# A chunked scan dealt out in five steps a unit between quarters of the projections

## The chip, the cores and the metric

The kernel runs on one core of a Trainium2 chip. Its time is the device time in microseconds (us) of one execution; three runs of the kernel before gave 2012.23, 2012.35 and 2016.85 us, a median of 2012.35. Six names stand for the engines: PE (matrix multiplication; PEld is its weight load), DVE (vector), ACT (activation functions, copies), POOL (GpSimd), and SP, which here issues nearly all DMAs. Each engine takes its instructions in a fixed order, in which an instruction that waits for a semaphore holds up all behind it.

## What is computed

One layer of a hybrid decoder, x of 2048 tokens by 1024, in float32:

```
u = rms_norm(x); proj = u @ w_in          # q, k, v, z_att, f, z_ssd, xbc, dt, x_lru, z_lru
y_att = fox_attention(q, k, v, log_f) * silu(z_att)       # 8 heads of 64
y_ssd = ssd_mixer(xbc, dt, z_ssd)                         # 16 heads in 2 groups, 16 chunks of 128
y_lru = rglru(x_lru) * silu(z_lru)
out = x + concat(y_att, y_ssd, y_lru) @ w_out
# ssd, per chunk c and group g, heads e:
lmat = exp(causal(a_cs[l] - a_cs[s])); cb = C_c @ B_c^T
y_diag = (cb * lmat_e) @ (x*dt)_e ; y_off = exp(a_cs) * (C_c @ state)
state  = exp(a_tot) * state + B_c^T @ (decay * x*dt)
```

## The kernel before

The stages follow each other: normalisation and transposes of x, convolution inputs, the gated linear recurrence and z_ssd, then the stage that the change is about, then attention with the output projection filled in between its steps. Tensors that pass between stages lie in DRAM (`xs_d`, `b_d`, `bt_d`, `ct_d`, `zs_d`, `acs_d`, the results `gt_d`, and q, k, v as `qk_d`, `v_d`).

In the stage around the change two things run side by side. **The scan** has 32 units (16 chunks by 2 groups), each made by `ssd_unit`: five loads (`xs`, `zz`, `bm`, `bt`, `ct`), the product `cb` on PE, two halves `q` of four heads each (load of the decays `ab`, a mask by POOL, four exponentials by ACT, a product with `cb` by DVE, four matmuls into `py`), the matmul `po` with the state, `y` on DVE, the matmul `pn` for the next state, and `store`: four transposes `pty`, a copy `yt` and the DMA to `gt_d`. `xs`, `bm`, `bt`, `ct`, `ab` and `y` have two buffers, `zz`, `xd`, `xe`, `yo` and `yt` one; the five PSUM results of a unit share three buffers (`psY`). **The projections** are 56 steps: 32 of q and k (`pqk`, in four groups of 8, each followed by transposes `ptq`, splits `sth` and `stl` on ACT and DVE, and four stores), 8 of v (`pv`), and 16 of z (`pza`). A group's weights come through four raw buffers `wr` and are split into `wh` and `wl` (eight buffers each), so the second half of the next group's weights can only be loaded when the group in progress is nearly over. In float32r a step of q/k has 48 matmuls of 256 columns, one of z 24 of 512.

The program writes the whole scan ahead of the projections, and a list scheduler with its own time model merges the two when the program is built: it takes what it thinks is ready, earlier text first. Nothing ties a unit of the scan to a projection step. What comes after the scan (`zm`, `q3`, `k2` and their memsets in the memory that the scan leaves) is written behind it, and the loads of attention's first head (`load_head(0)`, `load_q(0)`) stand behind the third group of projections.

Of the kernel before, what the change touches and what calls it, by code (L numbers as in the profile page):

```python
# [8 lines left out]
F32 = mybir.dt.float32  # L9
F32R = mybir.dt.float32r  # L10
# [33 lines left out]
UP, DOWN = (0, 1, 2, 3, 4, 5, 6, 7), (7, 6, 5, 4, 3, 2, 1, 0)  # L44
ORD = (DOWN,) + (UP,) * 6 + (DOWN,)
XB = 7
PB = (2, 3, 2, 1)


@with_exitstack  # L50
def hybrid_block(ctx, tc, x, norm_g, w_in, q_norm_g, k_norm_g, forget_b, ssd_conv_w, ssd_conv_b,
# [121 lines left out]
    for tb in range(4):  # L173
# [3 lines left out]
        ul.append([up.tile([P, 512], F32R, name=f"ul{tb}_{k}", tag=f"ul{tb}_{k}")  # L177
                   for k in range(KD)])

    gcount = [0]  # L180

    def weights(cols, rawp=wrp, eng=(V,)):

        n = sum(w for _, w in cols)
        i = gcount[0]
        gcount[0] += 1
        wh, wl = [], []
# [12 lines left out]
        return wh, wl, n  # L200
# [131 lines left out]
    def proj_tok2(w, t2, name, space=None):  # L332


        wh, wl, n = w
        pp, tag = space or (psj, "pj")
        ps = pp.tile([P, 2, 256], F32, name=name, tag=tag)
        for k in range(KD):
            for i in range(2):
                t = t2 * 2 + i  # L340
                h, l, sl = uh[t // 4], ul[t // 4], slice(t % 4 * P, t % 4 * P + P)
                last = k == KD - 1
                T.matmul(ps[:, i, :], h[k][:, sl], wh[k], start=(k == 0 and i == 0), stop=False,  # L343
                         skip_group_check=True)
# [7 lines left out]
    anchor = [None, None]  # L352

    def proj_ch(w, m, tb, name):
        wh, wl, n = w
        ps = psj.tile([P, 512], F32, name=name, tag="pj")
        ms = slice(m * P, m * P + P)
        for k in range(KD):
            T.matmul(ps, wh[k][:, ms], uh[tb][k], start=(k == 0), stop=False)  # L359
            T.matmul(ps, wh[k][:, ms], ul[tb][k], start=False, stop=False)  # L360
            ins = T.matmul(ps, wl[k][:, ms], uh[tb][k], start=False, stop=(k == KD - 1))  # L361
        anchor[0] = ins
        return ps

# [290 lines left out]
    sx = ExitStack()  # L655
    s1 = sx.enter_context(tpool(name="s1", bufs=1, side="right"))
    s2 = sx.enter_context(tpool(name="s2", bufs=2, side="right"))
    state = [None, None]

    def ssd_unit(c, g):  # L660
        u = f"{c}_{g}"
        tsl = slice(c * P, (c + 1) * P)
        hs = slice(g * 8, g * 8 + 8)
# [18 lines left out]
        py = psY.tile([P, 512], F32, name=f"py{u}", tag="Y")  # L682
# [16 lines left out]
        y = s2.tile([P, 8, 64], F32, name=f"y{u}", tag="y")  # L699
        y2 = y.rearrange("p h d -> p (h d)")  # L700
        G.tensor_tensor(xs, xs, drow[:, hs].unsqueeze(2).broadcast_to([P, 8, 64]), op=ALU.mult)
        V.tensor_tensor(y2, py, xs.rearrange("p h d -> p (h d)"), op=ALU.add)
        if state[g] is not None:
            po = psY.tile([P, 512], F32, name=f"po{u}", tag="Y")
            T.matmul(po, ct, state[g].rearrange("p h d -> p (h d)"), start=True, stop=True)
            yo = s1.tile([P, 8, 64], F32, name=f"yo{u}", tag="yo")
            V.tensor_tensor(yo, po.rearrange("p (h d) -> p h d", d=64),
                            eacs[:, c, hs].unsqueeze(2).broadcast_to([P, 8, 64]), op=ALU.mult)
            V.tensor_tensor(y, y, yo, op=ALU.add)
        V.tensor_tensor(y2, y2, zz, op=ALU.mult)  # L710
        sq = s1.tile([P, 512], F32, name=f"sqy{u}", tag="yo")
        A.activation(sq, y2, AF.Square, accum_out=rsn[:, c, g:g + 1])
        if c < NT - 1:
# [5 lines left out]
            else:  # L719
# [15 lines left out]
        return store  # L735

    store = None
    for c in range(NT):
        for g in range(2):
            nxt = ssd_unit(c, g)  # L740
            if store is not None:
                store()
            store = nxt
    store()

    rs2 = rsn.rearrange("p a b -> p (a b)")
    V.tensor_scalar(rs2, rs2, 1.0 / 512.0, 4.0 * EPS, op0=ALU.mult, op1=ALU.add)
    rsv = s1.tile([P, NT * 2], F32, name="rsv")
    V.tensor_copy(rsv, rs2)
    rsqrt(s2, rs2, rsv, NT * 2, "rg")  # L750
    sx.close()
    sgx.close()
    cx = ExitStack()
    kc = cx.enter_context(tpool(name="kc", bufs=1, side="right"))
    kvA = cx.enter_context(tpool(name="kvA", bufs=1, side="right"))
    units = [(h, sb) for h in range(8) for sb in ORD[h]]

    zm = kc.tile([P, 640], F32, name="zm")
    G.memset(zm, 0.0)
    G.affine_select(out=zm[:, 512:640], in_=zm[:, 512:640], pattern=[[-1, P]],  # L760
                    compare_op=ALU.is_ge, fill=-NEG, base=0, channel_multiplier=1)

    onr = kc.tile([P, 65], F32R, name="onr")
    G.memset(onr[:, 0:64].bitcast(F32), 0.0)
    G.memset(onr[:, 64:65].bitcast(F32), 1.0)
    idr = kc.tile([P, P], F32R, name="idr")
    V.tensor_copy(idr, ident)
    zmt = kc.tile([P, P], F32R, name="zmt")
    V.tensor_scalar(zmt, tri, NEG, -NEG, op0=ALU.mult, op1=ALU.add)

    q3s, qxs = [], []

    def make_q(pool):
        i = len(q3s)
        q3 = pool.tile([P, 512], F32R, name=f"q3{i}")
        G.memset(q3[64:128, :].bitcast(F32), 0.0)
        G.memset(q3[64:66, :].bitcast(F32), 1.0)
        q3s.append(q3)  # L780
        qxs.append(pool.tile([P, 512], F32R, name=f"qx{i}"))

    for i in range(2):
        make_q(kc)
    k2s = {}

    def make_k2(b):
        k2 = (kvB if b else kvA).tile([P, S], F32R, name=f"k2{b}")
        G.memset(k2[64:128, :].bitcast(F32), 0.0)
        G.memset(k2[96:97, :].bitcast(F32), -1.0)  # L790
        k2s[b] = k2

    make_k2(0)
    heads = {}
    qs_ = {}

    def load_head(h):
        p, b = divmod(h, 2)
# [14 lines left out]
    def load_q(j):  # L813
# [49 lines left out]

    with tpool(name="ap", bufs=2) as pool, tpool(name="ap1", bufs=1) as ap1, \
            tpool(name="qkp", bufs=QB) as qkp:
        for p in range(4):
            w = weights([(C_Q + p * P, P), (C_K + p * P, P)])
            for th in range(8 // NQ):  # L870
# [453 lines left out]
```

## Time and profile before

| what | before |
|---|---|
| median of 3 runs | 2012.35 us |
| profiled execution | 2011.36 us, of which the span of instructions is 2009.5 |
| PE busy | 1946.7 us (97% of the span) |
| DVE, ACT, POOL busy | 1296.2, 1005.0, 807.9 us |
| DMA | 130 GB/s on average, 169 between 745 and 1260 us |

All times inside the program count from the span's start. The scan runs from about 750 to 1131 us, the projections from about 752 to 1250. PE's busy time is not its work alone: matmuls overlap, and one that starts behind a wait, or under a lower granted clock, lasts longer.

### The profile page before, as it was taken

The numbers are of one execution on the slowest core, as the hardware profiler recorded it, in microseconds if no ns is written. First come the engines' busy times: TensorE is split into PE (matmuls) and PEld (weight loads), VectorE is DVE, ScalarE is ACT, GpSimd is POOL, SyncE is SP. The second block draws the span as 40 slices with busy tenths as digits, with TensorE's granted clock in tenths as the row PEclk, the third lists the DMA queues.
The fourth block names the chain that finished last, engine by engine and source line by source line (L and its number), as shares of the span: only waits on it lengthen the run. The fifth ranks groups of instructions, "written<-read, shape, count | busy, mean of one in ns | idle before, by whom it ended". The sixth has DMA issues, their size and how long they took to land.

```text
span 2009.5 us, 34885 instructions
## 1 busy us (share of the span) xinstructions
PE 1946.7 (97%) x11941; PEld 1705.1 (85%) x11941; DVE 1296.2 (65%) x2573; ACT 1005.0 (50%) x2174; POOL 807.9 (40%) x920
## 2 busy tenths in 40 slices
PE   7999999999999999899999999999999999998899
PEld 6898888898989899787888897888899888887787
DVE  6748555573645556767667534788788887896333
ACT  7625444453544544444444333576777776675010
POOL 0100000232222224445555200687888887786110
PEclk9999999999999999999999999999999999999999
DMA  5332223121212135657666724765565764523353
GB/s 191 84 100 67 70 74 105 48 65 43 70 38 75 32 114 140 185 169 209 206 198 175 197 81 141 217 166 156 164 169 163 196 161 143 173 83 113 123 173 126
DMA packets 260032, 261.30 MB, mean 130 GB/s; under 512 B 26724, under 2 KB 198016, under 8 KB 258304
## 3 DMA queue, kind: packets, MB, share of 16 engines
q1 hardware_dynamic: 259696, 259.05, 43.7%
q8 instruction: 95, 1.56, 0.3%
q0 software_dynamic: 160, 0.03, 0.1%
q14 instruction: 81, 0.66, 0.1%
HBM read 164.22 MB, written 94.77 MB: 129 GB/s over the span
## 4 chain that ended last, share of the span: by engine, by line
PE 44%; DMA 3%; DVE 2%; issue 1%; ACT 1%; POOL 1%; SPq 1%; DVEq 0%; POOLq 0%; ACTq 0%
PE po L1145 6%; PE po L1146 5%; PE po L1147 5%; PE T L1011 3%; PE T L1012 3%; PE O L1067 3%; PE O L1069 3%; PE S L970 3%; PE pza L360 1%; PE pza L361 1%; PE pza L359 1%; PE pqk L345 1%; PE pqk L343 1%; PE pqk L347 1%; DMA ab<-acs_d 1%
## 5 line engine op out<-in xcount | busy, mean ns | idle before, releaser
L1145 PE MATMUL po<-woh,mh 128*128 128x512 f32 x512 | 204.9, 400 | 13.9 <-DVE xo L1151 11.4
L1024 DVE TENSOR_TENSOR pl<-T,ph 128x512 fp32r<-128x512 f32 (+1 forms) x288 | 185.5, 652 | 38.9 <-ACT T L1023 32.7
L1146 PE MATMUL po<-wol,mh 128*128 128x512 f32 x512 | 202.4, 395 | 0.0
L1147 PE MATMUL po<-woh,ml 128*128 128x512 f32 x512 | 201.7, 395 | 0.0
L1022 ACT ACTIVATE ph<-T 128x512 fp32r<-128x512 f32 (+1 forms) x288 | 165.4, 574 | 51.0 <-PE T L1012 43.5
L1037 POOL TENSOR_TENSOR ac<-ac,ph 128x512 f32<-128x512 f32 x120 | 158.7, 1323 | 23.8 <-ACT ph L1022 18.1
L1023 ACT ACTIVATE T<-T 128x512 f32<-128x512 f32 (+1 forms) x288 | 164.7, 572 | 0.3
L359 PE MATMUL pxx<-uh,wh 128*128 128x512 f32 x384 | 152.8, 400 | 1.1 <-ACT uh L304 1.0
L360 PE MATMUL pxx<-ul,wh 128*128 128x512 f32 x384 | 153.1, 400 | 0.0
L361 PE MATMUL pxx<-uh,wl 128*128 128x512 f32 x384 | 150.9, 395 | 0.0
L347 PE MATMUL pqk<-wh,ul 128*128 128x256 f32 x512 | 150.9, 295 | 0.0
L980 DVE TENSOR_REDUCE mc<-S 128x1 f32<-128x512 f32 x192 | 128.5, 682 | 32.4 <-PE S L970 30.7
L1067 PE MATMUL O<-ph,vv 128*128 128x256 f32 (+1 forms) x576 | 148.1, 278 | 0.6 <-ACT ph L1022 0.5
L1011 PE MATMUL T<-q,k 128*128 128x256 f32 x576 | 146.3, 279 | 2.1 <-ACT q L995 1.6
L345 PE MATMUL pqk<-wl,uh 128*128 128x256 f32 x512 | 148.3, 290 | 0.0
L343 PE MATMUL pqk<-wh,uh 128*128 128x256 f32 x512 | 147.8, 289 | 0.0
L420 DVE SCALAR_TENSOR_TENSOR accx<-rtx,cv,accx 128x512 f32<-128x512 f32 x144 | 108.3, 753 | 57.7 <-ACT accx L417 54.7
L345 PE MATMUL pzs<-wl,uh 128*128 128x256 f32 x512 | 143.6, 281 | 0.0
L347 PE MATMUL pzs<-wh,ul 128*128 128x256 f32 x512 | 143.3, 281 | 0.0
L343 PE MATMUL pzs<-wh,uh 128*128 128x256 f32 x512 | 143.0, 281 | 0.0
L1012 PE MATMUL T<-qx,kx 128*128 128x256 f32 x576 | 142.7, 279 | 0.0
L1069 PE MATMUL O<-pl,vv 128*65 128x256 f32 x576 | 141.4, 277 | 0.0
(357 smaller groups left out, 5693.2 us busy)
## 6 DMA issues: line engine op xcount, KB each, us to landing
ab<-acs_d SPq DMA_DIRECT2D x64, 256.0 KB
pt_d<-xr SPq DMA_DIRECT2D x64, 256.0 KB
wr<-in_w_in_dram SPq DMA_DIRECT2D x112, 128.0 KB
xt<-in_x_dram SPq DMA_DIRECT2D x16, 512.0 KB
xs_d<-stx SPq DMA_DIRECT2D x32, 256.0 KB
v_d<-vs SPq DMA_DIRECT2D x32, 256.0 KB
wr<-in_w_in_dram SPq DMA_DIRECT2D x128, 64.0 KB
zs_d<-zs SPq DMA_DIRECT2D x32, 256.0 KB
```

What stands on the lines that cost most here:

```text
L343: T.matmul(ps[:, i, :], h[k][:, sl], wh[k], start=(k == 0 and i == 0), stop=False, skip_group_check=True)
L345: T.matmul(ps[:, i, :], h[k][:, sl], wl[k], start=False, stop=False, skip_group_check=True)
L347: ins = T.matmul(ps[:, i, :], l[k][:, sl], wh[k], start=False, stop=last, skip_group_check=True)
L360: T.matmul(ps, wh[k][:, ms], ul[tb][k], start=False, stop=False)
L1011: T.matmul(ps, k2[:, ks], q3[:, qs], start=(jj == 0), stop=False, skip_group_check=True)
L1012: ins = T.matmul(ps, kx[:, ks], qx[:, qs], start=False, stop=True, skip_group_check=True)
L1024: marks["V"].append(V.tensor_tensor(pl[:, 0:n], pt[:, 0:n], ph[:, 0:n].bitcast(F32), op=ALU.subtract))
L1067: T.matmul(po[:, qs], vv[:, kt, 0:128], ph[:, cs], start=(kt == 0), stop=(kt == 2 * sb + 1), skip_group_check=True)
L1069: T.matmul(po[0:65, q2], vv[:, kt, 64:129], pl[:, cs], start=False, stop=False, skip_group_check=True)
L1145: T.matmul(ps, mh[:, j, :], h, start=(j == 0), stop=False)
L1146: T.matmul(ps, mh[:, j, :], l, start=False, stop=False)
L1147: T.matmul(ps, ml[:, j, :], h, start=False, stop=(j == 3))
```

## The change

`ssd_unit` becomes a generator of five steps: (1) loads, `cb`, masks, exponentials and products; (2) the `gt_d` DMA of the store before, `po`, `yo`; (3) the first half of `py`; (4) the second half; (5) `y`, `pn`, state, and the transposes and the copy of the unit before. The decays `ab` get four buffers. `proj_tok2` and `proj_ch` call `tick` after every second of their eight k, so a projection step has four ticks; `scan` takes the next scan step when `done[1] * 184 < done[0] * 160`: 160 steps on 184 ticks, 46 projection steps. Each step's PE instructions are held behind that tick's matmul (`issue_after`, an order on PE alone) and all its instructions, like the weights of the stage, get a high priority. When the scan is over, `begin` frees its memory, writes the memsets and calls `load_head(0)` and `load_q(0)`.

```diff
+SPAN = 184
@@ weights
+        if between[0] is not None:
+            with tc.high_priority(offset=HP):
+                return split_weights(cols, rawp, eng, i, n)
@@ proj_tok2, proj_ch
+            if k % 2:
+                tick(ins)
@@ ssd_unit
-            ab = s2.tile([P, 4, P], F32, name=f"ab{u}_{q}", tag="ab")
+            ab = s4.tile([P, 4, P], F32, name=f"ab{u}_{q}", tag="ab")
...
-            for e in range(4):
-                o = (q * 4 + e) * 64
-                T.matmul(py[:, o:o + 64], ab[:, e, :], xd[:, q * 4 + e, :], start=True, stop=True)
+            abs_.append(ab)
+        yield
+        last[1]()
         if state[g] is not None:
             po = psY.tile([P, 512], F32, name=f"po{u}", tag="Y")
...
+        yield
+        py = psY.tile([P, 512], F32, name=f"py{u}", tag="Y")
+        for q, ab in enumerate(abs_):
+            for e in range(4):
+                o = (q * 4 + e) * 64
+                T.matmul(py[:, o:o + 64], ab[:, e, :], xd[:, q * 4 + e, :], start=True, stop=True)
+            yield
...
+        before()
...
-            dma(gt_d[g][:, :, tsl].rearrange("i p t -> p i t"), yt)
+            last[1] = lambda: dma(gt_d[g][:, :, tsl].rearrange("i p t -> p i t"), yt)
@@ the last projections
+        def scan(ins):
+            done[0] += 1
+            while done[1] >= 0 and done[1] * SPAN < done[0] * 160:
+                done[1] += 1
+                with tc.high_priority(offset=HP), tc.issue_after(ins.ins):
+                    if next(ssd, 0) == 0:
+                        done[1] = -1
+                if done[1] < 0:
+                    begin()
...
-            if p == 2:
-                load_head(0)
-                load_q(0)
+        between[0] = None
```

Outside this stage the order of PE's instructions is the same in both programs, and the number of instructions is the same on every engine. Three places show what the order has become. Names are those of the code with chunk and group (`py5_0` is chunk 5, group 0) and a running number.

PE, unit 5_0, before; the rows left out are projection matmuls: 27, 6, 11 and 4 of them.

```order
L675 MATMUL cb5_0_8054<-ct5_0_8048,bt5_0_8047 128x128
...
L698 MATMUL py5_0_8060<-xd5_0_8056,ab5_0_0_8061 128x64 x4
L705 MATMUL po5_0_8092<-st0_0_7435,ct5_0_8048 128x512
...
L698 MATMUL py5_0_8060<-xd5_0_8056,ab5_0_1_8075 128x64 x4
L715 MATMUL pn5_0_8100<-xe5_0_8058,bm5_0_8046 128x512
...
L730 MATMUL pty4_1_8104<-ident_102,y4_1_8021 128x128 x4
...
L675 MATMUL cb5_1_8122<-ct5_1_8116,bt5_1_8115 128x128
```

The same unit on PE now; left out are 13, 13, 10, 24 and 12 projection matmuls.

```order
L694 MATMUL cb5_0_9225<-ct5_0_9219,bt5_0_9218 128x128
...
L720 MATMUL po5_0_9264<-st0_0_7573,ct5_0_9219 128x512
...
L729 MATMUL py5_0_9280<-xd5_0_9227,ab5_0_0_9231 128x64 x4
...
L729 MATMUL py5_0_9280<-xd5_0_9227,ab5_0_1_9241 128x64 x4
...
L742 MATMUL pn5_0_9338<-xe5_0_9229,bm5_0_9217 128x512
L758 MATMUL pty4_1_9342<-ident_102,y4_1_9185 128x128 x4
...
L694 MATMUL cb5_1_9371<-ct5_1_9365,bt5_1_9364 128x128
```

A unit now has 72 projection matmuls from one `cb` to the next, and 48 before; `po` stands ahead of `py`, and the two halves of `py` stand apart from `po` and `pn`.

POOL around the same unit, before (`AFFINE_SELECT` is the mask of the decays, `xd` the input of `py`):

```order
L689 AFFINE_SELECT ab5_0_0_8061<-ab5_0_0_8061 128x512
L677 TENSOR_TENSOR xd5_0_8056<-xs5_0_8044,dt_117 128x512
L680 TENSOR_TENSOR xe5_0_8058<-xs5_0_8044,dec_212 128x512
L689 AFFINE_SELECT ab5_0_1_8075<-ab5_0_1_8075 128x512
L701 TENSOR_TENSOR xs5_0_8044<-xs5_0_8044,drow_111 128x512
L721 TENSOR_TENSOR st0_0_7435<-st0_0_7435,etot_118 128x512
```

and now:

```order
L708 AFFINE_SELECT ab5_1_0_9377<-ab5_1_0_9377 128x512
L696 TENSOR_TENSOR xd5_0_9227<-xs5_0_9215,dt_117 128x512
L708 AFFINE_SELECT ab5_1_1_9387<-ab5_1_1_9387 128x512
L699 TENSOR_TENSOR xe5_0_9229<-xs5_0_9215,dec_212 128x512
L733 TENSOR_TENSOR xs5_0_9215<-xs5_0_9215,drow_111 128x512
L748 TENSOR_TENSOR st0_0_7573<-st0_0_7573,etot_118 128x512
```

Beside the work of unit 5_0 now stand the masks of the next unit, 5_1; before it was its own.

SP at the end of the scan, before (`k20`, `kx0`, `vv0`, `q30`, `qx0` are the loads of attention's first head, `wr21` the weights of the last eight steps of z); the rows left out hold other stores and the weights of the fourth q/k group:

```order
L733 DMA gt_d1_96<-yt15_1_9533 128x4x128
...
L905 DMA kl_d2_74<-stl2_7_1_12084 128x256
L805 DMA k20_9581<-kh_d0_68 64x2048
...
L809 DMA vv0_12378<-v_d_76 128x16x128
L820 DMA q30_9573<-qh_d0_60 64x512
L821 DMA qx0_9576<-qh_d0_60 64x512
...
L194 DMA wr21_4_13076<-in_w_in_dram 128x256
```

and now, where only `kx0` and two stores are left out:

```order
L761 DMA gt_d1_96<-yt15_1_12813 128x4x128
...
L956 DMA kl_d3_75<-stl3_3_1_12602 128x256
L798 DMA k20_12862<-kh_d0_68 64x2048
...
L802 DMA vv0_12866<-v_d_76 128x16x128
L813 DMA q30_12854<-qh_d0_60 64x512
L814 DMA qx0_12857<-qh_d0_60 64x512
L209 DMA wr21_4_13080<-in_w_in_dram 128x256
```

The first head's loads moved from behind the third group of q/k to directly ahead of the second half of the last weights. On PE, 84 `pqk` and 36 `pza` matmuls stand between the scan's last transposes (`pty15_1`) and the first matmul with `wh21_4`.

## Rows read from the trace of the kernel before

**Rows 1.** Windows: start:end, length, busy PE, PEld, DVE, ACT, POOL, PEclk, DMA, GB/s.
```profile
745.00:1120.00 375.00, 351.34 (x2543) 311.07 (x2542) 254.16 (x431) 173.65 (x487) 179.52 (x181) 0.98 0.62 180
...
800.00:850.00 50.00, 44.96 (x333) 39.91 (x334) 38.82 (x68) 24.22 (x67) 24.06 (x26) 1.00 0.65 186
```

**Rows 2.** Lines, 745 to 1260 us: busy, mean ns, then PE's idle time before them.
```profile
L698 PE MATMUL py<-xd,ab 128*128 128x64 f32 x512 | 66.9, 277 | 17.1 <-DVE ab L694 6.7 <-issue 3.1 <-POOL xs L701 2.6
...
L730 PE MATMUL pty<-ident,y 128*128 128x128 f32 x128 | 19.6, 275 | 2.5 <-DVE yo L707 1.4 <-DVE y L702 1.1
...
L895 PE MATMUL ptq<-ident,qk 128*128 128x128 f32 x128 | 18.9, 274 | 2.3 <-DVE stl L902 2.3
...
L675 PE MATMUL cb<-ct,bt 128*128 128x128 f32 x64 | 13.2, 288 | 1.8 <-DVE y L702 1.7
```

**Rows 3.** Chain of waits, in order of time: start, us, what.
```profile
948.98 2.52 DMA ql_d<-stl
...
968.67 4.50 DMA ab<-acs_d
973.29 0.65 POOL ab L689
973.96 1.29 ACT ab L693 x4
975.33 0.70 DVE ab L694
976.07 1.10 PE py L698 x8
...
986.52 0.84 PE py L698 x8
```

**Rows 4.** Waits, 745 to 1260 us: total, times, longest.
```profile
ACT ab L693 <- POOL ab L689: 103.6, 43, 6.4
POOL ab L689 <- DMA ab<-acs_d: 54.5, 29, 6.4
...
ACT sth L901 <- DMA kh_d<-sth: 24.9, 9, 4.6
...
PE py L698 <- DVE ab L694: 6.7, 6, 1.9
```

**Rows 5.** Waits of SP's queue, 745 to 1300 us.
```profile
SPq L686 <- PE py L698: 50.8, 34, 3.1
```

**Rows 6.** Windows, PE alone: busy, granted clock, DMA share, GB/s.
```profile
875.00:880.00 5.00, 2.35 (x14) 0.81 0.50 166
880.00:885.00 5.00, 5.00 (x18) 0.50 0.19 66
...
975.00:980.00 5.00, 3.93 (x13) 0.71 0.67 173
...
1095.00:1100.00 5.00, 4.24 (x13) 0.66 0.66 188
```

**Rows 7.** Timeline of PE: start, length, instruction.
```profile
1000.42 0.28 PE L347 MATMUL pv<-wh,ul 128*128 128x256 f32 x1
...
1002.18 0.28 PE L347 MATMUL pv<-wh,ul 128*128 128x256 f32 x1
```

**Rows 8.** Chain of waits around the scan's end.
```profile
1131.04 0.44 PE pty L730 x4
...
1133.78 0.24 PE pza L360
```

**Rows 9.** Timeline of SP's queue.
```profile
1134.15 0.39 SPq L733 DMA_DIRECT2D gt_d<-yt  x1
...
1136.78 0.46 SPq L805 DMA_DIRECT2D k<-kh_d  x1
...
1139.20 7.54 SPq L820 DMA_DIRECT2D q<-qh_d  x1
1146.80 0.59 SPq L821 DMA_DIRECT2D qx<-qh_d  x1
```

More of the change, by code (lines that the diff above doesn't have):

```diff
@@ L178, in hybrid_block, with tick @@
                    for k in range(KD)])
+    anchor = [None, None]
+    between = [None]
+    def tick(ins):
+        if between[0] is not None:
+            between[0](ins)
     gcount = [0]
@@ L186, in weights, with split_weights @@
         gcount[0] += 1
+        if between[0] is not None:
+            with tc.high_priority(offset=HP):
+                return split_weights(cols, rawp, eng, i, n)
+        return split_weights(cols, rawp, eng, i, n)
+    def split_weights(cols, rawp, eng, i, n):
         wh, wl = [], []
@@ L348, in proj_tok2 @@
                                skip_group_check=True)
+            if k % 2:
+                tick(ins)
         anchor[0] = ins
         return ps
-    anchor = [None, None]
     def proj_ch(w, m, tb, name):
@@ L361, in proj_ch @@
             ins = T.matmul(ps, wl[k][:, ms], uh[tb][k], start=False, stop=(k == KD - 1))
+            if k % 2:
+                tick(ins)
         anchor[0] = ins
@@ L657, in hybrid_block, with ssd_unit @@
     s2 = sx.enter_context(tpool(name="s2", bufs=2, side="right"))
+    s4 = sx.enter_context(tpool(name="s4", bufs=4, side="right"))
     state = [None, None]
-    def ssd_unit(c, g):
+    def ssd_unit(c, g, before):
         u = f"{c}_{g}"
@@ L681, in ssd_unit @@
                             op=ALU.mult)
-        py = psY.tile([P, 512], F32, name=f"py{u}", tag="Y")
+        abs_ = []
         for q in range(2):
             qs = slice(g * 8 + q * 4, g * 8 + q * 4 + 4)
-            ab = s2.tile([P, 4, P], F32, name=f"ab{u}_{q}", tag="ab")
+            ab = s4.tile([P, 4, P], F32, name=f"ab{u}_{q}", tag="ab")
             dma(ab.rearrange("p h l -> p (h l)"),
@@ L708, in ssd_unit @@
                             eacs[:, c, hs].unsqueeze(2).broadcast_to([P, 8, 64]), op=ALU.mult)
+        yield
[5 more added lines that the diff above has]
+            yield
+        y = s2.tile([P, 8, 64], F32, name=f"y{u}", tag="y")
+        y2 = y.rearrange("p h d -> p (h d)")
+        G.tensor_tensor(xs, xs, drow[:, hs].unsqueeze(2).broadcast_to([P, 8, 64]), op=ALU.mult)
+        V.tensor_tensor(y2, py, xs.rearrange("p h d -> p (h d)"), op=ALU.add)
+        if state[g] is not None:
             V.tensor_tensor(y, y, yo, op=ALU.add)
@@ L732, in store @@
             A.copy(yt, pt)
-            dma(gt_d[g][:, :, tsl].rearrange("i p t -> p i t"), yt)
[L735 to L749, printed above, removed]
@@ L750, in hybrid_block, with ssd_steps @@
-    rsqrt(s2, rs2, rsv, NT * 2, "rg")
-    sx.close()
-    sgx.close()
+            last[1] = lambda: dma(gt_d[g][:, :, tsl].rearrange("i p t -> p i t"), yt)
+        last[0] = store
+    last = [lambda: None, lambda: None]
+    def ssd_steps():
+        for c in range(NT):
+            for g in range(2):
+                yield from ssd_unit(c, g, last[0])
+                yield
+        last[1]()
+        last[0]()
+        last[1]()
+        rs2 = rsn.rearrange("p a b -> p (a b)")
+        V.tensor_scalar(rs2, rs2, 1.0 / 512.0, 4.0 * EPS, op0=ALU.mult, op1=ALU.add)
+        rsv = s1.tile([P, NT * 2], F32, name="rsv")
+        V.tensor_copy(rsv, rs2)
+        rsqrt(s2, rs2, rsv, NT * 2, "rg")
@@ L753, in hybrid_block @@
     cx = ExitStack()
-    kc = cx.enter_context(tpool(name="kc", bufs=1, side="right"))
-    kvA = cx.enter_context(tpool(name="kvA", bufs=1, side="right"))
     units = [(h, sb) for h in range(8) for sb in ORD[h]]
[L758 to L793, printed above, removed]
+    kp_ = {}
     heads = {}
     qs_ = {}
+    q3s, qxs = [], []
+    k2s = {}
     def load_head(h):
@@ L823, in load_q, with make_q, make_k2, begin @@
         qs_[j // 2] = q3, qx
+    kc = kvA = kvB = zm = onr = idr = zmt = None
+    def make_q(pool):
+        i = len(q3s)
+        q3 = pool.tile([P, 512], F32R, name=f"q3{i}")
+        G.memset(q3[64:128, :].bitcast(F32), 0.0)
+        G.memset(q3[64:66, :].bitcast(F32), 1.0)
+        q3s.append(q3)
+        qxs.append(pool.tile([P, 512], F32R, name=f"qx{i}"))
+    def make_k2(b):
+        k2 = (kvB if b else kvA).tile([P, S], F32R, name=f"k2{b}")
+        G.memset(k2[64:128, :].bitcast(F32), 0.0)
+        G.memset(k2[96:97, :].bitcast(F32), -1.0)
+        k2s[b] = k2
+    def begin():
+        nonlocal kc, kvA, zm, onr, idr, zmt
+        sx.close()
+        sgx.close()
+        kc = cx.enter_context(tpool(name="kc", bufs=1, side="right"))
+        kvA = cx.enter_context(tpool(name="kvA", bufs=1, side="right"))
+        zm = kc.tile([P, 640], F32, name="zm")
+        G.memset(zm, 0.0)
+        G.affine_select(out=zm[:, 512:640], in_=zm[:, 512:640], pattern=[[-1, P]],
+                        compare_op=ALU.is_ge, fill=-NEG, base=0, channel_multiplier=1)
+        onr = kc.tile([P, 65], F32R, name="onr")
+        G.memset(onr[:, 0:64].bitcast(F32), 0.0)
+        G.memset(onr[:, 64:65].bitcast(F32), 1.0)
+        idr = kc.tile([P, P], F32R, name="idr")
+        V.tensor_copy(idr, ident)
+        zmt = kc.tile([P, P], F32R, name="zmt")
+        V.tensor_scalar(zmt, tri, NEG, -NEG, op0=ALU.mult, op1=ALU.add)
+        for i in range(2):
+            make_q(kc)
+        make_k2(0)
+        load_head(0)
+        load_q(0)
     def load_wo(ws, k0, half, last, behind=()):
@@ L867, in hybrid_block @@
             tpool(name="qkp", bufs=QB) as qkp:
+        ssd = ssd_steps()
+        done = [0, 0]
+        def scan(ins):
[7 more added lines that the diff above has]
+                    begin()
+        between[0] = scan
         for p in range(4):
```

4 lines of the change are left out of this document (removed).

## The prediction, made before the changed kernel ran

> **What bounds the kernel now.** I read the windows first, because the share of busy time is an average over stages: between 745 and 1120 us, where the scan runs beside the projections, PE is busy for 351.3 of 375 us [rows 1]. So in this stage PE is the bound and still loses time; no other engine is busy for more than 68% of it (DVE, 254 of 375). The lines tell before which instruction PE sat: 17.1 us before the matmuls `py`, 2.5 before the transposes `pty`, 2.3 before `ptq`, 1.8 before `cb`, together 23.7 [rows 2], which is all that the window lacks (375 - 351.3).
>
> The chain of waits tells why `py` is late. One half-unit reads: load of the decays 4.50 us, mask 0.65, exponentials 1.29, product 0.70, then `py` [rows 3], 7.4 us in series from the load on. The load can't be early, because `ab` has two buffers: SP stood 50.8 us waiting for a `py` that freed one [rows 5], POOL 54.5 us for the load, ACT 103.6 us for POOL [rows 4]. The scan runs in a loop of latencies, and PE, whose order is fixed, meets a `py` too soon. Those waits show as 6 of 1.1 us on average where DVE came last [rows 4]; at that mean 17.1 us are about 15 waits.
>
> Two further losses hang on these waits. Eight instructions of `py` take 1.10 us behind a wait and 0.84 in a run [rows 3], so each costs 0.26 more, 15 of them 3.9 us. [...] What is lost is 5 x (0.19 + 0.50 + 0.29 + 0.34) = 6.6 us. The stage loses 23.7 + 3.9 + 6.6 = 34.2 us. Its other 341 us are work that both programs have.
>
> **The change, part by part.**
>
> *Four places of decays, and products a unit ahead.* On POOL the masks of the next unit now stand beside the work of this one, so the loop of 7.4 us has a whole unit: 72 projection matmuls, at (1002.18 - 1000.42) / 15 = 0.117 us [rows 7], are 8.4 us, and the unit's own PE work comes on top (two halves of `py` alone 1.7 us). The waits for the load, the mask and the exponentials should go. What remains between `cb` and `py` is DVE's product, 0.70 us, against 26 matmuls (3.0 us) and `po`. Late next is DVE itself, whose order is fixed too: a split `stl` that waits for an earlier store holds the product behind it, as the longest wait of ACT's `sth` for a store (4.6 us [rows 4]) shows. Waits whose last cause was DVE's product were 6.7 of the 17.1 us; I let half of them stay, 3.3 us in 3 waits. Ends: all 17.1 + 3.9 = 21.0 us go, or half of it, 10.5. I take 21.0 - 3.3 - 0.8 = 16.9 us gained.
>
> *Steps tied to quarters of a projection.* `pty` comes a unit later than its `y`, and `cb` and `ptq` find DVE less blocked by products that wait for ACT. Their 6.6 us of waits [rows 2] go between not at all and wholly; nothing in the rows says which, so I take half: 3.3 us.
>
> *Clock.* The three falls stand behind long waits for `py`; with the waits the falls go. I take all 6.6 us, with 3.3 as the low end.
>
> *Stores a unit late, weights early, splitting `po` from `py`.* The `gt_d` store leaves `yt` occupied longer, but ACT copies only once in a unit, hidden by 72 matmuls; if SP is late, ACT waits and costs nothing until its exponentials have lost their unit of lead. PE runs from one kind of matmul into the other without a gap (rows 7 follow a `pn`), so more switches cost nothing that the trace shows.
>
> *The end of the scan.* It comes later: its last transposes ended at 1131.5 [rows 8], over 100 us before the projections were through; now 84 `pqk` and 36 `pza` matmuls separate them from the first use of `wh21_4`: 84 x 0.117 + 36 x 0.24 [rows 7, 8] = 18.5 us. The loads of the first head now stand on SP ahead of that weight. Before, the first of them was issued 5.3 us behind the last transposes (1136.8), and SP was then stuck for 7.54 us in issuing `q`; the one after, `qx`, was through at 1147.4 [rows 9], 10.6 us after the first. Nothing stood behind it then that PE needed soon. Now: 5.3 us at the least; nearer 8, since the stores of two transposed tiles stand between, each waiting for an earlier store to land (2.52 us [rows 3]) before its buffer is free; then 10.6; then 2.5 for the weight's own landing at the quickest, some 2 more because `vv` is still under way. That is 23 us against 18.5, a wait of about 4.5 us. It is long enough for one fall of the clock, by rows 6 a third of 6.6, 2.2 us. So 6.7 us lost; ends 0 (5.3 + 10.6 + 2.5 = 18.4 us) and 10.9 (5.3 + 4.6 us ahead of the loads give a wait of 6.5, and the clock falls for twice as long).
>
> [...]
>
> *The sum.* 16.9 + 3.3 + 6.6 - 6.7 = 20.1 us less. Against the profiled execution, 2011.36 us, that gives 1991.3; the median of the runs shown is 1.0 above it, so I predict 1992 us. From the next stage on PE's order is unchanged, so nothing is given back there.
>
> **The rivals.**
>
> *All hidden.* Every wait of the scan stage goes and the weight is there in time: 34.2 us less, 1978. For it: a unit's PE work and 72 matmuls exceed each chain that the trace shows. Against: DVE is as busy a share as before, and the store waits of `sth` and `stl` are untouched.
>
> *The weights late by more.* If the first head's loads go out 13 us behind the last transposes, the wait is 10 us and the clock falls for twice as long (4.4): 14.4 instead of 6.7, so 2000. For it: SP's order, where all of it stands in one file. Against: 13 us are more than any wait in rows 4.
>
> *Slower: PE held at each of the new places.* A step's PE work can't slide any more: five places a unit, each with its own wait, in a fixed order with the projections. If DVE, with products, sums and splits in one queue, is late at one place in each unit by 1.2 us (the longest such wait now is 1.9 [rows 4]), that is 32 x (1.2 + 0.26) = 46.7 us of waits and, at the clock's loss per idle us of before (6.6 / 23.7 = 0.28), 10.7 us of clock: 57.4 in place of 34.2, and 6.7 for the weight: 2042. It decides from 0.5 us a unit on: 32 x (0.5 + 0.26 + 0.14) + 6.7 = 35.5.
>
> *Clock.* Short waits spread evenly could let the clock fall more often although they sum to less: three falls more than I keep are 6.6 us, 1999. Between 800 and 850 us PE lost 5.0 of 50 us in shorter waits and the granted clock stayed at 1.00 [rows 1], so I hold this unlikely. [...]
>
> *It only moves the waits.* With SP, DVE and ACT as serial as before, waits for `ab` come back as waits for stores, and the time stays: 2011.
>
> **How the numbers follow.** Chances: the forecast 0.47, all hidden 0.16, weights 0.14, clock 0.06, waits moved 0.07, slower 0.10. My terms' ends give 34.2 at best (1978) and 10.5 + 0 + 3.3 - 10.9 = 2.9 us at worst (2009); a range of 1980 to 2007 leaves the slower case, the moved waits and a tip of the hidden case outside. The forecast's own range is 1984 to 2001. What a measurement can tell from no change is about 0.3%, 6 us: faster means below 2006.3. Forecast, hidden, weights and clock fall there but for some 0.04 of the last two and the forecast's tail: faster 0.79; within 0.3% 0.11; slower 0.10.
>
> **What would show it.** Between 750 and 1195 us PE should be idle for 3 to 10 us in all, `py` hardly among the waiters, and the clock at full speed; SP should no longer wait for `py`, nor ACT for POOL. The scan should end near 1195 us and one wait before `pza` with a weight as its releaser should follow it, with a fall of the clock. I am wrong if `py` or `cb` still wait in most units for DVE, if that wait at `pza` exceeds 10 us, or if time is lost in the attention stage.

## The result, and the profile after

The changed kernel takes 1999.6 us (median of six runs, 1996.8 to 2006.6) against 2012.3; the ratio is 0.9946, with a 95% interval of 0.9931 to 0.9962. That is 12.7 us less; 20 were forecast. The profiled execution took 1999.03 us with a span of 1997.2, so it is 12.3 us below the profiled one of before.

The gain sits in the scan stage. From the first matmul of `pqk` to the first score `S` PE needed 481.5 us before and needs 467.6 now, 13.9 less. Outside it little differs: the stage began 2.0 us later (756.4 against 754.4), behind a PE order that is the same, and from the first `S` to the end it took 773.1 us against 773.7. The later start is not the change's work as far as the traces show: in the changed kernel's profiled run the granted clock was 0.74 and 0.92 between 35 and 45 us, which costs 5 x (0.26 + 0.08) = 1.7 us, and before it was 1.00 there. So the stage gained more than the whole.

The windows of the stage, changed kernel (start:end, length, busy PE, PEld, DVE, ACT, POOL, PEclk, DMA, GB/s):

```profile
745.00:1120.00 375.00, 359.50 (x2603) 320.85 (x2603) 231.36 (x419) 168.16 (x466) 156.47 (x165) 1.00 0.58 175
745.00:1195.00 450.00, 434.50 (x3168) 390.21 (x3168) 279.18 (x522) 200.72 (x549) 183.46 (x195) 1.00 0.58 171
...
1200.00:1205.00 5.00, 4.05 (x11) 3.18 (x12) 4.01 (x11) 1.52 (x4) 0.00 (x0) 0.66 0.86 235
```

The first line answers to the first of [rows 1]: PE is busy for 8.2 us more of the same 375, and DVE for less, because its work is spread over a longer stretch. The second says that the stage still has 15.5 us of idle PE, and the granted clock is at 1.00 throughout. The one fall on the way to the first score (0.66 in 5 us) stands behind the weights.

PE's lines between 745 and 1260 us (busy, mean ns | idle time before them and who ended it), for [rows 2]:

```profile
L729 PE MATMUL py<-xd,ab 128*128 128x64 f32 x512 | 63.6, 269 | 0.9 <-DMA qh_d<-sth 0.4 <-issue 0.2 <-DVE ab L713 0.2
L374 PE MATMUL pza<-uh,wh 128*128 128x512 f32 x128 | 52.8, 413 | 2.4 <-ACT wh L211 2.4
...
L720 PE MATMUL po<-st,ct 128*128 128x512 f32 x60 | 31.2, 602 | 5.5 <-DVE st L750 5.5
L758 PE MATMUL pty<-ident,y 128*128 128x128 f32 x128 | 19.2, 272 | 0.0
L946 PE MATMUL ptq<-ident,qk 128*128 128x128 f32 x128 | 19.0, 276 | 7.7 <-DVE stl L953 5.4 <-DVE qk L941 2.3
L694 PE MATMUL cb<-ct,bt 128*128 128x128 f32 x64 | 12.6, 279 | 1.0 <-DVE y L734 1.0
```

The idle time before `py` fell from 17.1 us to 0.9 and that before `pty` from 2.5 to none. But `po`, which had no line among the waiters before, now waits 5.5 us, `ptq` 7.7 instead of 2.3. The waits of these two are all for DVE.

Why `po` waits, at the longest of its five waits, in the chain of waits (start, us, what):

```profile
781.32 0.86 PE po L720 x2
...
934.78 0.39 ACT ab L712
935.16 0.37 ACT sth L952
...
935.56 0.03 DVE stl L953
935.59 0.37 issue
935.96 0.69 DVE st L750
...
936.69 1.13 PE po L720 x2
```

And in DVE's timeline (start, length, instruction, in brackets the idle time before it):

```profile
935.56 0.48 DVE L953 SCALAR_TENSOR_TENSOR stl<-ptq,cv,sth 128x256 fp32r<-128x256 f32 x1 [2.20 <-ACT sth L952]
935.96 0.68 DVE L750 TENSOR_TENSOR st<-st,pn 128x512 f32<-128x512 f32 x1
```

`po` takes the PSUM place that `pn` held, and `pn`, which had ended at 931.4, is read by DVE's `st`. `st` stood in DVE's queue behind a split `stl` which waited 2.20 us for ACT's `sth`, and ACT came to `sth` late because it stood at the exponentials of `ab`. The first line of the chain is a `po` in a run: 0.86 us, 0.27 less than behind the wait.

The other four waits have the same last step, `st` late in DVE's queue, but not all the same cause. At 1054.33 `po` waits 1.72 us, because `st` stands behind a split of the weights, `wl`, for which ACT's `wh` was late, again behind the exponentials (ACT's and DVE's timelines):

```profile
1051.65 1.28 ACT L712 ACTIVATE ab<-ab,nacs 128x128 f32<-128x128 f32 x4 [4.87 <-POOL ab L708]
...
1053.25 0.42 DVE L212 TENSOR_TENSOR wl<-wr,wh 128x256 fp32r<-128x256 f32 x1 [3.63 <-ACT wh L211]
```

Before a third (0.80 us) a `stl` had waited 2.79 us for its store, and before the last two (0.70 and 0.55) DVE had only been busy. So ACT at the exponentials stands behind 3.5 of the 5.5 us.

The three queues off PE's path, 745 to 1260 us (total, times, longest):

```profile
SPq L705 <- PE py L729: 46.9, 31, 3.6
...
ACT ab L712 <- POOL ab L708: 114.4, 38, 7.8
POOL ab L708 <- DMA ab<-acs_d: 103.2, 32, 7.3
...
DVE stl L953 <- ACT sth L952: 20.7, 16, 4.2
...
DVE stl L953 <- DMA kl_d<-stl: 17.0, 11, 2.8
...
DVE stl L953 <- DMA ql_d<-stl: 5.6, 7, 1.4
```

Against [rows 4, 5]: SP stands at the decays' loads for `py` nearly as long as before (46.9 us against 50.8), POOL waits for them longer (103.2 against 54.5), and ACT behind POOL too (114.4 against 103.6). Four places hide these waits from `py`; they do not end them.

The end of the scan in SP's timeline:

```profile
1184.40 0.45 SPq L798 DMA_DIRECT2D k<-kh_d  x1
...
1188.22 6.50 SPq L813 DMA_DIRECT2D q<-qh_d  x1
...
1195.47 2.21 SPq L209 DMA_DIRECT2D wr<-in_w_in_dram  x4
```

The same stretch in the chain of waits:

```profile
1179.93 0.33 PE pty L758 x3
...
1195.47 5.00 DMA wr<-in_w_in_dram
1200.49 0.41 ACT wh L211
1200.95 0.50 PE pza L374
```

The last `pty` ends at 1180.3, the head's loads begin 4.1 us later, the weights 11.1 behind these, the first lands in 5.0, and `pza` waits 2.4 us.

### The profile page after: what moved, and what is told of

Same layout as the page of the kernel before. It is cut to its first block, busy times and chain, and to the rows that moved or that the text cites. A ratio compares the mean times of both kernels' runs of the same rounds, so it can differ in the third digit from the quotient of the medians.

```text
span 1997.2 us, 34858 instructions
## 1 busy us (share of the span) xinstructions
PE 1940.4 (97%) x11941; PEld 1700.7 (85%) x11941; DVE 1283.2 (64%) x2573; ACT 1003.4 (50%) x2174; POOL 802.2 (40%) x920
## 4 chain that ended last, share of the span: by engine, by line
PE 87%; DMA 5%; DVE 3%; ACT 2%; issue 1%; SPq 1%; POOL 0%; DVEq 0%; POOLq 0%; ACTq 0%
PE po L1194 6%; PE po L1195 6%; PE po L1196 6%; PE pxx L375 4%; PE pxx L376 4%; PE pxx L374 4%; PE T L1060 3%; PE T L1061 3%; PE pzs L360 3%; PE pzs L358 3%; PE pzs L362 3%; PE O L1116 3%; PE S L1019 3%; PE O L1118 3%; PE pqk L358 2%; PE pqk L360 2%
## 5 line engine op out<-in xcount | busy, mean ns | idle before, releaser
L1194 PE MATMUL po<-woh,mh 128*128 128x512 f32 x512 | 205.4, 401 | 13.0 <-DVE xo L1200 10.6
L1073 DVE TENSOR_TENSOR pl<-T,ph 128x512 fp32r<-128x512 f32 (+1 forms) x288 | 185.5, 652 | 38.9 <-ACT T L1072 32.6
L1086 POOL TENSOR_TENSOR ac<-ac,ph 128x512 f32<-128x512 f32 x120 | 158.6, 1321 | 22.6 <-ACT ph L1071 17.4
L358 PE MATMUL pqk<-wh,uh 128*128 128x256 f32 x512 | 155.3, 304 | 0.0
L712 ACT ACTIVATE ab<-ab,nacs 128x128 f32<-128x128 f32 x256 | 82.9, 392 | 124.2 <-POOL ab L708 123.9
L362 PE MATMUL pqk<-wh,ul 128*128 128x256 f32 x512 | 144.2, 282 | 0.0
```

Source lines behind the costliest of these rows:

```text
L1194: T.matmul(ps, mh[:, j, :], h, start=(j == 0), stop=False)
```

## The experiments

Theory after the result: the places of `ab` and the dealing both take `py`'s wait away; what is left hangs on DVE's fixed order, which stands behind `stl`, `sth` and their stores, and on the weights behind the first head's loads. Each row of the table is from the profile of one kernel: its median and ratio to the kernel before, the time from the first `pqk` to the first `S`, PE's idle time in us before the instructions named (745 to 1260 us), and what the clock lost before the first `S` (5 us times what is missing to 1.00, summed over windows of 5 us).

```
kernel           median   ratio to before         pqk-S  py   po   ptq  pty  cb   pza  clock
before           2012.3                           481.5  17.1  -   2.3  2.5  1.8   -   6.8
changed          1999.6   0.9946 [0.9931,0.9962]  467.6  0.9  5.5  7.7   -   1.0  2.4  1.7
e_ab2            2005.1   0.9962 [0.9947,0.9976]  471.6  3.6  7.5  4.3   -   0.8  3.3  5.1
e_before_ab4     2003.1   0.9960 [0.9946,0.9974]  472.2  4.8  0.5   -   9.9  1.5  2.5  1.7
e_storenow       1999.2   0.9938 [0.9925,0.9951]  469.6  0.5  7.8  5.4   -   1.1  1.8  5.1
e_span160        2002.8   0.9960 [0.9945,0.9975]  475.9  6.5  7.4  8.2   -   0.3   -   5.1
e_head           2001.0   0.9948 [0.9927,0.9968]  466.2  2.2  4.7  8.6   -   0.7   -   1.7
e_pty            1996.1   0.9924 [0.9902,0.9946]  464.4  0.4  3.2  6.5   -   0.7  2.7  5.1
e_stl3ab3        2000.0   0.9935 [0.9914,0.9956]  470.6  2.0  6.1  5.1   -    -   2.4  6.8
e_abpool         1992.5   0.9905 [0.9889,0.9921]  461.0   -   4.2  2.9   -   1.8  2.8  5.1
e_pool_pty       1994.1   0.9906 [0.9890,0.9922]  464.8  2.0  1.3  6.9   -   1.7  3.4  3.4
e_best           1993.7   0.9895 [0.9877,0.9913]  461.9  1.4   -   8.2   -   1.8   -   5.1
e_pool_head      1991.0   0.9892 [0.9874,0.9911]  463.6   -   6.5  5.4   -   1.1   -   6.9
e_before_ab4pool 2012.8   1.0002 [0.9985,1.0019]  481.4  4.0   -   8.3  8.0  3.8   -  10.2
```

The runs of one kernel lie up to 17 us apart, so medians 3 us apart tell nothing alone; the waits of the traces are read beside them. Two cautions go with that. The ratios compare better than the medians, because the kernel before was run again beside each group of experiments and its median there lies between 2010.3 and 2012.5. And the waits are those of one execution a kernel, which can lie off the median: that of `e_span160` took 2009.42 us at a median of 2002.8, that of `e_pool_head` 1995.41 at 1991.0, that of `e_head` 1994.36 at 2001.0.

**One part of the change at a time.** The dealing without the places (`e_ab2`), and the places without the dealing (`e_before_ab4`):

```
-    s4 = sx.enter_context(tpool(name="s4", bufs=4, side="right"))
+    s4 = sx.enter_context(tpool(name="s4", bufs=2, side="right"))
```

> The changed kernel with the decays back in two places instead of four, all else of the change kept. Theory 1 (the four places made the gain): a new load of decays must again wait for py of the unit before, 4.5 + 0.65 + 1.3 + 0.7 = 7.2 us pass until the next py, and py waits again for DVE: 10 to 17 us of idle PE before py, 2009 to 2016 us. Theory 2 (the even dealing made it): py of one unit and py of the next stand 11.2 us apart now (46 projection steps over 32 units), which is 4 us more than the 7.2 of that chain, so that py waits under 4 us in all: 2000 to 2004 us.

```
+    s4 = sx.enter_context(tpool(name="s4", bufs=4, side="right"))
-            ab = s2.tile([P, 4, P], F32, name=f"ab{u}_{q}", tag="ab")
+            ab = s4.tile([P, 4, P], F32, name=f"ab{u}_{q}", tag="ab")
```

> The kernel before with the decays in four places, and nothing else of the change. Theory 1 (the four places made the gain): the loads go out a unit earlier, the 17.1 us of waits before py and the clock's 6.6 us with them shrink to a quarter, 1995 to 2001 us. Theory 2 (the even dealing made it): py still stands right behind its own masks on PE whatever the load does, and of the 17.1 us more than half stay: 2006 to 2012 us.

Each alone takes most of `py`'s wait away: 17.1 us fall to 3.6 by the dealing and to 4.8 by the places. So for `py` theory 2 holds in the first run and theory 1 in the second, and by the time the first lies next to theory 2's range and the second between the two: either part is enough. In the stage they are worth 9.9 and 9.3 us, together 13.9, less than the sum. By the time it is not shown that the two together beat one of them, since the intervals of the three ratios overlap. "The dealing" is here all of the change but the places: the order of the steps, the hold behind a tick's matmul and the high priority, which no run took apart. What differs is what is left. PE's lines with the places alone:

```profile
L699 PE MATMUL py<-xd,ab 128*128 128x64 f32 x512 | 61.3, 273 | 4.8 <-issue 2.7 <-POOL xs L702 1.9
...
L731 PE MATMUL pty<-ident,y 128*128 128x128 f32 x128 | 19.9, 278 | 9.9 <-DVE y L703 9.8
```

And with the dealing alone:

```profile
L729 PE MATMUL py<-xd,ab 128*128 128x64 f32 x512 | 64.6, 272 | 3.6 <-DVE rqk L126 1.6 <-ACT yt L760 1.2 <-ACT vs L398 0.5
...
L720 PE MATMUL po<-st,ct 128*128 128x512 f32 x60 | 31.2, 602 | 7.5 <-DVE st L750 7.5
```

Without the dealing `pty` comes too soon behind DVE's `y`; the dealing ends that (no `pty` waits in any kernel that has it) and pays with `po` and `ptq`.

**The late store undone** (`e_storenow`):

```
-            last[1] = lambda: dma(gt_d[g][:, :, tsl].rearrange("i p t -> p i t"), yt)
+            dma(gt_d[g][:, :, tsl].rearrange("i p t -> p i t"), yt)
```

> The changed kernel with the store of gt issued right behind the copy yt again, not one unit late. Theory (the late store keeps SyncE from standing at yt): SyncE waits 1 to 3 us longer for yt in each of some 30 units, the stores of sth and stl and the loads behind them come later, and ptq and po wait 1 to 4 us more in all: 2000.5 to 2004 us. Rival: SyncE already waits for yt in 19 units (32.8 us), so the place hardly matters: 1998.5 to 2000.5 us.

The rival holds: 1999.2 against 1999.6. This part of the change moves nothing that can be measured.

**The pace** (`e_span160`):

```
-SPAN = 184
+SPAN = 160
```

> The changed kernel with the scan's steps dealt over 40 projection steps instead of 46. Theory (the distance between a producer on DVE or a store and PE's use of it sets the waits): 32 units stand about 13% closer, the waits for st and stl (10.9 us) grow by a third or more, +3 to +6 us, against 4 us for the weights that are no longer behind the head's loads: 1998 to 2003 us, with more PE idle in the scan stage. Rival (the waits are bursts that the distance doesn't change): only the 4 us of the weights' wait go: 1995 to 1997 us.

The theory's figure came, 2002.8 us, but only half of its reason. The weights' wait is gone, and PE is idle for longer at `py`, `po` and `ptq`:

```profile
L729 PE MATMUL py<-xd,ab 128*128 128x64 f32 x512 | 64.4, 272 | 6.5 <-DVE ab L713 2.6 <-POOL xs L733 1.7 <-ACT yt L760 1.2
...
L720 PE MATMUL po<-st,ct 128*128 128x512 f32 x60 | 32.7, 627 | 7.4 <-DVE st L750 7.2
...
L946 PE MATMUL ptq<-ident,qk 128*128 128x128 f32 x128 | 19.8, 282 | 8.2 <-DVE qk L941 4.2 <-DVE stl L953 4.0
```

The waits that were to grow, those for `st` and `stl`, did not: 7.2 + 4.0 = 11.2 us against 10.9. What grew is `py`, from 0.9 to 6.5. That fits a distance between a product and its use that counts, but at another place than the theory had it, in a profiled run 6.6 us above the kernel's median, and the intervals of the two ratios overlap.

**The weights** (`e_head`; the first head's loads are tied behind the last weight load):

```
-        load_head(0)
-        load_q(0)
...
         w = weights([(C_ZA + g * 256, 256)])
+        if g == 1:
+            with tc.high_priority(offset=HP), tc.issue_after(gin[0].ins):
+                load_head(0)
+                load_q(0)
```

> The changed kernel with the first head's loads (k, kx, vv, q, qx) issued behind the last four weight loads instead of ahead of them. Theory: the 2.40 us wait of pza for wh and the half clock behind it (about 1.7 us) go, 4 us less, 1995 to 1996.5 us. Rival: the head's last load then lands when the scores want it, the wait moves to S, no gain: 1999 to 2003 us.

The wait of `pza` is gone and no score waits for the head, so the place was read rightly. A wait of the same kind, 2.5 us, stands in the table for `e_before_ab4`: there the head's loads went out ahead of weights of the first eight steps of z. So such a wait does not need the dealing. By the time it is open: the runs fall into two groups (two at 1994, five at 1999.9 to 2003.7), and in the trace, which is of a run at 1994, `ptq` took back some of it, in one wait of 2.79 us with a fall of the clock behind it.

**`po`'s PSUM place** (`e_pty`):

```
+        before()
         if c < NT - 1:
             pn = psY.tile([P, 512], F32, name=f"pn{u}", tag="Y")
...
-        before()
```

> The changed kernel with the transposes pty of the unit before ahead of pn instead of behind it, so that po takes the PSUM place that pty left (freed by ACT's copy) and no longer the one of pn (freed by DVE's add st). Theory: the 5.5 us of po's waits for st and the slow po behind them (5 times 0.26 us) go, 5 to 7 us less: 1993 to 1995 us. Rival: DVE stands behind its stl and wl either way, and py or the next cb, which take the place of pn now, wait in po's stead: 1998 to 2001 us.

Between the two. `po`'s line in this kernel:

```profile
L720 PE MATMUL po<-st,ct 128*128 128x512 f32 x60 | 30.9, 597 | 3.2 <-ACT yt L760 2.4 <-DVE st L751 0.8
```

`po`'s waits for `st` fall from 5.5 to 0.8 us, but 2.4 us for ACT's `yt` take their place. So the mechanism is shown: who frees the place decides whom `po` waits for. The size is not: the median is 1996.1, 3.5 less, and the intervals of the two ratios overlap.

**More places for the splits** (`e_stl3ab3`; the decays give up one place for the room):

```
-    s4 = sx.enter_context(tpool(name="s4", bufs=4, side="right"))
+    s4 = sx.enter_context(tpool(name="s4", bufs=3, side="right"))
...
+            tpool(name="qkp", bufs=QB) as qkp, tpool(name="sp3", bufs=3) as sp3:
...
-                        sl = pool.tile([P, 256], F32R, name=f"stl{p}_{t2}_{j}", tag="stl")
+                        sl = sp3.tile([P, 256], F32R, name=f"stl{p}_{t2}_{j}", tag="stl")
```

> The changed kernel with three places for stl instead of two; the decays have three places instead of four, which pays for the room. Theory A (DVE stands still because a place of stl comes free only when its store has landed, and ptq and po's st stand behind it): DVE's waits for stores before stl fall from 22.6 us to under 8, ptq's waits for stl from 5.4 to under 1.5 us, and po's for st go down with them from 5.5: 4 to 7 us less, 1993 to 1996 us. Rival: the stores keep DVE just as long and the third place only shifts the wait to sth or to py, whose decays have a place less: 1999 to 2002 us.

Theory A gets its first step and not its gain. The waits of DVE and ACT around the splits:

```profile
DVE stl L953 <- ACT sth L952: 32.8, 28, 4.8
ACT sth L952 <- DMA qh_d<-sth: 13.9, 14, 3.3
...
ACT sth L952 <- DMA kh_d<-sth: 12.0, 8, 3.4
...
DVE stl L953 <- DMA kl_d<-stl: 4.0, 1, 4.0
```

DVE's waits for stores fall from 22.6 us to 4.0, and its waits for `sth`, which still has two places, rise from 20.7 to 32.8. The rival, that the wait shifts to `sth`, is what happened: 2000.0 us. The decays' third place in place of the fourth cost little beside it: `py` waits 2.0 us, 1.1 more.

**SyncE freed of the decays' loads** (`e_abpool`):

```
-            dma(ab.rearrange("p h l -> p (h l)"),
+            G.dma_start(ab.rearrange("p h l -> p (h l)"),
```

> The changed kernel with the loads of the decays issued by GpSimd instead of SyncE. Theory B (the stores of stl are late because SyncE stands 46.9 us at loads of decays that wait for py, with the stores behind them): ptq's waits for stl and part of po's for st go, 4 to 7 us less, 1993 to 1996 us. Theory A (the time until a store has landed is what stl waits for, whoever issues what): those waits stay at 4 to 6 us, and GpSimd, which now waits for py itself, holds its masks and state products: 1999 to 2005 us.

The time of theory B came, 1992.5 us, with an interval clear of the changed kernel's. Its reason did not. The waits in this kernel:

```profile
POOL ab L708 <- DMA ab<-acs_d: 38.9, 43, 3.5
...
POOL ab L705 <- issue: 30.0, 12, 3.9
...
POOL ab L705 <- PE py L729: 28.4, 4, 22.6
...
DVE stl L953 <- DMA ql_d<-stl: 14.9, 10, 2.9
DVE stl L953 <- DMA kl_d<-stl: 14.3, 11, 4.3
ACT ab L712 <- POOL ab L708: 12.7, 19, 1.7
DVE stl L953 <- ACT sth L952: 11.8, 15, 1.6
```

DVE waits longer for stores than in the changed kernel (29.2 us against 22.6), so the stores were not what came sooner. Nor is SP free: what it no longer waits at the decays it waits at the loads of `xs`, 74.9 us against 10.1 in the changed kernel:

```profile
SPq L688 <- DVE y L734: 74.9, 22, 7.2
```

What fell is POOL's wait for the decays (103.2 to 38.9), with it ACT's for the masks (114.4 to 12.7), and DVE's for ACT's `sth` (20.7 to 11.8). ACT, which has the exponentials and `sth` in one queue, is the link that fits, as in the chain at 935 us and at 1052 us above; no run changed it alone, so this cause is argued and not shown.

**Together** (`e_pool_pty`, `e_best`, `e_pool_head`: the edits of `e_abpool`, `e_pty` and `e_head` combined).

> The changed kernel with the decays' loads issued by GpSimd and pty ahead of pn. Theory (two separate holds: SyncE at the decays' loads for the stores, DVE's st for po's place): the gains add, 7 us (1992.5 with GpSimd's loads alone) and 3.5 us (1996.1 with pty alone) off 1999.6: 1987.5 to 1991 us, no po waiting for st. Rival (one hold, seen twice: what frees DVE also brings st early): 1991 to 1994 us.

> As the run before this one, and the first head's loads behind the last weights too. Theory: the wait of pza for wh and the half clock behind it go as well, 3 to 4.5 us less than without: 1984 to 1987.5 us. Rival: with the scan's end 6 us earlier the weights or the head are late at another place, no gain: 1988 to 1991 us.

> The changed kernel with the decays' loads issued by GpSimd and the first head's loads behind the last weights, pty where the change has it. Theory (the weights' wait is a loss of its own): 2.8 us of waiting and the half clock behind it go from what GpSimd's loads alone reach (461.0 us from the first pqk to the first score, 1992.5 us): 456 to 458 us there, 1987.5 to 1990 us. Rival (what is won at one of these waits is given back at ptq, which waits for stl): 460 to 463 us there, 1991 to 1994 us.

With `pty` ahead of `pn` no `po` waits for `st` any more, but `ptq` waits 6.9 us instead of 2.9, and the time does not fall: here the rival, one hold seen twice, is right. PE's `ptq` line in `e_pool_pty`:

```profile
L946 PE MATMUL ptq<-ident,qk 128*128 128x128 f32 x128 | 19.1, 276 | 6.9 <-DVE stl L953 6.2 <-DVE qk L941 0.7
```

The head behind the weights takes the wait of `pza` away in both kernels that have it. The medians fall by 0.4 us (`e_best` against `e_pool_pty`) and 1.6 us (`e_pool_head` against `e_abpool`), which the spread of the runs does not tell from nothing. `e_best` lies above both of its expectations. `e_pool_head` lies by its median between theory and rival, and by the stage of its profiled run, 463.6 us against the 461.0 without the edit, just above the rival: what `pza` no longer waits, `po` and `ptq` wait. The four that have the dealing and GpSimd's loads, `e_pool_head`, `e_best`, `e_abpool` and `e_pool_pty`, are about 1% faster than the kernel before and beat the changed one; between them the runs do not choose.

**GpSimd's loads without the dealing** (`e_before_ab4pool`):

> The kernel before with the decays in four places and their loads issued by GpSimd, without the dealing. Theory (the dealing's own part is the distance between a unit's last product y and its pty): the 9.8 us of pty's waits for y stay, SyncE's part of the rest goes: 1999 to 2003 us. Rival (with four places and a free SyncE the dealing is worth nothing): 1992 to 1996 us.

Both expectations missed: 2012.8 us, 9.7 more than with SyncE's loads. The waits of POOL, and those of DVE and PE at the splits:

```profile
POOL ab L687 <- PE py L699: 81.6, 23, 19.5
...
DVE stl L903 <- DMA ql_d<-stl: 21.3, 10, 10.3
...
PE ptq L896 <- DVE stl L903: 7.5, 2, 6.2
```

`pty`'s wait for `y` stays (8.0 us), as the theory had it; but one `ptq` waits 6.2 us, and the granted clock falls more. Against the kernel with SyncE's loads the stage is 9.2 us longer; the clock lost 8.5 us more (10.2 against 1.7) and PE sat 4.9 us more before the instructions of the table.

Why the same edit gained with the dealing and lost without it is not shown. POOL stands at a decays' load in both: 29 times for 100.2 us here, 23 of them by the profile for `py`, and 30 times for 89.5 us in `e_abpool`, where the profile names another releaser or none ("issue") for most. Behind the first load of the scan, for which POOL stands 19.5 and 22.6 us, the longest such wait is 10.4 us here and 3.9 there. That would fit a `py` that frees its place earlier under the dealing. What held the one store for 10.3 us stays open.

## Why the prediction was right, and where it was not

*Four places of decays: right, and more than counted.* `py`'s idle time fell by 16.2 us where I had counted 13.8 (17.1 less 3.3 that DVE should keep); DVE kept 0.2. With the 3.9 us of slow `py` behind waits that is 20.1 in place of 16.9; the 3.9 are taken over from the forecast, and `py`'s busy time fell by 3.3 (66.9 to 63.6). `e_before_ab4` shows that this part alone does it, and `e_ab2` that the dealing would have done it too.

*Steps tied to quarters: the step that failed.* I let half of the 6.6 us at `pty`, `cb` and `ptq` go. `pty`'s went, but `ptq` rose by 5.4 and `po`, which I gave no price, came in with 5.5: 6.6 became 14.2, a loss of 7.6 and not a gain of 3.3. The rival with PE held at its new places had the mechanism: 14.2 us over 32 units are 0.44 us each, near the 0.5 from which I let it decide. It did not decide because the waits were 15 and not 32, so that fewer slow starts came with them, and in the profiled run no fall of the clock. I had named a cause, a `stl` that waits and holds DVE, but tied it to `ab` alone; I did not ask which reader frees the PSUM place that `po` takes.

*Clock: right in the profiled run, in part by luck.* The forecast's 6.6 us are 5 us times what the granted clock lacks in the four windows of [rows 6], which show three falls. All 6.6 went from the scan (the table has 6.8, with a fifth window at 0.95). It is the least certain term: `e_storenow`, the changed kernel but for one store, lost 3.4 us there by two falls. One of them came behind two waits of `ptq`, 0.74 and 0.79 us, where the changed kernel's two, at the same place, were 0.57 and 0.79 and had none. The changed kernel itself has 15.5 us of idle PE between 745 and 1195, in waits of up to 1.75 us, and a granted clock of 1.00 there.

*Weights: place right, size 4.1 us and not 6.7.* The distance from the last `pty` to the first use was 18.3 us (18.5 forecast) and the head's loads took 11.1 (10.6); they began 4.1 us behind `pty`, not 8. The wait was 2.4 and the clock lost 1.7. The weight landed 5.00 us behind its issue, near the 4.5 of the forecast. That it did not pass `vv` can be read from SP's queue, where the load at L815, which starts at 1198.96, had waited for `vv`:

```profile
SPq L815 <- DMA vv<-v_d: 0.9, 1, 0.9
```

So `vv` landed at about 1198.9 and the first weight at 1200.5; why in this order is not shown. The wait of 6.5 us at the forecast's upper end came from loads that begin 9.9 us behind `pty`; they began 4.1 behind, and the wait was 2.4.

*The sum* with these sizes: 20.1 - 7.6 + 6.6 - 4.1 = 15.0, less what `po` and `ptq` lose by starting slowly behind 13 waits. `po` loses 0.27 us (1.13 against 0.86, above), `ptq` by the same chain 0.22 (0.66 against 0.44): 5 x 0.27 + 8 x 0.22 = 3.1. That leaves 11.9.

That this is so near the 12.3 measured for the whole execution is chance. The terms are all of the stage, and the stage gained 13.9: 2.0 us of it stand in none of them and stay open. The whole has 12.3 because the stage began 2.0 us later, behind the fall of the clock at 35 to 45 us, and 0.6 came back after it. The forecast of 20.1 came within 8 us because terms erred both ways: 3.2 us too little for `py` and 2.6 too much for the weights, against 10.9 too much at the quarters and 3.1 of slow starts that it did not have.

*What would show it.* Idle PE was 15.5 us, not 3 to 10, and the scan's last `pty` ended at 1180, not near 1195. The statement that SP would no longer wait for `py`, nor ACT for POOL, was plainly wrong, and `e_abpool`, in which SP's wait is gone and ACT's is 12.7 us, is 7 us faster.

## What to carry to other kernels

More buffers and an earlier place are two cures for one wait: price them together, not as a sum (either alone took `py`'s 17.1 us down to 4.8 or 3.6), and look at the waits behind the buffers, which here stayed (POOL's 103.2 us for the loads) or moved to another instruction of the same queue (SP's 74.9 us at `xs` in `e_abpool`). When a step gets a new place in a fixed order, list for each PSUM place who frees it and what stands ahead of that reader in its queue; here that was for the longest waits a split, `stl` or `wl`, waiting for ACT. A load that waited for a place kept its queue standing in these runs (SP for 46.9 us in the changed kernel, POOL for 89.5 in `e_abpool`), so which queue that should be is to be measured and not assumed: on GpSimd it gained 7 us with the dealing and cost 10 without, and the waits on record do not say why.

## What the runs showed of the hardware

SP needed 6.50 us to issue the small load `q` (128 KB) behind 2.5 MB of the head's loads, 7.30 with the weights ahead of them (`e_pool_head`, `q` at 1188.37) and 7.54 before [rows 9]. What stands next in SP's order, `qx`, went out 6.56, 7.35 and 7.60 us behind the start of `q`. What SP stood for in that time no trace shows.

A long wait cost PE twice more in these traces: the matmuls behind it started slowly (`po` 1.13 us against 0.86 in the changed kernel's chain of waits, above), and the clock fell behind some. PE's timeline in `e_abpool`:

```profile
929.96 2.07 PE L720 MATMUL po<-st,ct 128*128 128x512 f32 x2 [2.96 <-DVE st L750]
```

And in `e_head`:

```profile
1074.34 0.63 PE L949 MATMUL ptq<-ident,qk 128*128 128x128 f32 x4 [2.79 <-DVE stl L956]
```

The granted clock was 0.72 in the window of 5 us from 930 and 0.66 in the one from 1075. The 0.50 that [rows 6] has for a whole window stands in the changed kernel's fall behind the weights too: in windows of 0.5 us it was 0.50 from 1201.5 to 1204.5 us and 1.00 from 1205 on. The changed kernel's waits of up to 1.75 us in the scan had no fall behind them. But the length of a wait does not settle it: in `e_abpool` a wait of 2.06 us (`ptq`, at 1030) had no fall behind it, and before one of 1.59 us (`py`, at 1095.76) had one; nor did the pair of short waits in `e_storenow` differ much from the pair without a fall in the changed kernel. So the idle time of these traces does not give the clock's loss, which has to be read from the granted clock, run by run.
